# Two head pairs and a quarter of the frames in each step of an RWKV-7 recurrence, prepared further ahead

## The chip, the cores and the metric

The kernel runs on one core of one Trainium2 chip. The metric is device time in microseconds (us) for one execution, as a median over runs. Of the core's engines, TensorE (PE in the rows; PEld is its weight load) multiplies matrices into PSUM, VectorE (DVE) and ScalarE (ACT) work element by element and empty PSUM, GpSimd (POOL) helps with both kinds of elementwise work that touch no PSUM, and SyncE (SP) issues the DMAs, in the order in which they stand in the program.

## The reference

One residual block of a streaming encoder, on 1024 frames of 1024 channels, all in float32:

```python
h    = rmsnorm(x);  proj = h @ w_in                  # columns r | k | v | glu | gate logits
rkv  = rkv + (token_shift(rkv) - rkv) * mu_rkv
a    = rwkv7_mixer(h, r, k, v, ...)                  # 16 heads of 64, the recurrence below
c    = conformer_conv_mixer(glu)                     # GLU, causal depthwise conv of width 31, LayerNorm, silu
merged = gates[0] * (a @ w_rwkv_proj) + gates[1] * (c @ w_conv_proj)
x    = x + merged @ w_out
x    = x + square(relu(rmsnorm(x) @ w_ff1)) @ w_ff2
out  = rmsnorm(x)

def frame_step(S, r_t, w_t, k_t, v_t, kk_t, a_t):    # one head, S is 64 x 64
    sa = einsum('vk,k->v', S, -kk_t)
    S  = S * w_t + outer(sa, kk_t * a_t) + outer(v_t, k_t)
    return S, einsum('vk,k->v', S, r_t)
```

Decay `w_t`, rate `a_t` and the gate of the mixer come from small two-layer projections of h. Each head's output is normalised over its 64 channels, scaled, and given a bonus term of r, k and v.

## The kernel before

Activations lie channels by frames. A wide product is made of float32r products: both operands are split into a high and a low part, and each 128x128 block of weights (`whi`, `wlo`) is multiplied by 512 frames (`hhi`, `hlo`) three times. These are the "wide products" of the text: in the rows they write tile `g` and have form 128x512. Half a unit (four blocks, two segments of 512 frames) is 24 of them; a unit, 48, gives 128 columns of `w_in`.

The recurrence is computed in chunks of 64 frames. A head pair is 128 channels; two heads h lie on the partitions 0-63 and 64-127. There are 8 head pairs, and before the change a **step** i takes one head pair and half of the frames, that is 8 chunks, so there are 16 steps. For each step the following generators issue their work:

- `prep` makes decay products, the normalised key `kk` and the bonus `bn`. It reads k, r and v from SBUF, where `u_rkv` left them, and loads z and a (`z_d`, `al_d`) from DRAM. It contains two head sums (`headsum`, two 512-wide products each, tile `l`).
- `front` (twice per step, q = 0 and 1, four chunks each) transposes (`pt`) and makes for each head the products `pg` (4 calls of contraction 64, output 128x128). ScalarE and VectorE empty them into `lt`, `pl` and `mr`.
- `v_tm` transposes v (`pv`) into the tiles `sav` and `stv`.
- `invert` inverts the 64x64 triangular matrices of the step: 16x16 blocks by GpSimd, through DRAM (`scr_l`, `scr_x`, `scr_z`), and then TensorE (`pi`, `px`, `pz`, `pt2`, `pz2`).
- `chain` carries the state over the chunks, one after the other. Per chunk, for two heads: `ps1 = pl x stv` and the first half of the output `po = pr x stv`; VectorE copies ps1 to `rs`, and ScalarE makes `stw = stv * wc`; `ps2 = z x rs`, which VectorE copies into `sav`; `ps3 = bkt x sav`, from which VectorE makes the next state, `stv = ps3 * wc + stw`, and the second half of the output, `po += mr x sav`.
- `group_norm` normalises the output of the step (two head sums) and stores it (`a_d`).

The order of all engines in this stage is the order in which the program issues: a fixed dependency is added between an engine's consecutive instructions. The program goes through **ticks**. A step is NT = 24 ticks; `PLAN` says at which tick of which step a generator starts, each `yield` is one tick, and `chain` uses three ticks per chunk. After the generators of a tick, `large` issues wide products until the priced work of TensorE reaches TICK = 1800 (ns by a price list in the program) times the number of ticks, and `conv_ops` issues operations of the depthwise convolution on VectorE until its priced work has used a share DSHARE = 0.75 of the tick, at most two per tick. So the wide products (the columns r, k, v, glu and gates of `w_in`) fill the time in which the recurrence waits. Wide products not needed at a certain time (gates) go last; what is left of them is used after the recurrence. Before the loop of steps there are only four ticks for the second layer of the decay and rate projections (`second_layer`, tile `za`).

PSUM: three banks for the wide products, one for head sums, two (`mp`, tag "m") for all tiles of front, v_tm and invert, one for ps1 to ps3 and one for po.

## Time and profile before

| | |
|---|---|
| median of 3 runs | 2155.57 us (2146.05 to 2156.53) |
| profiled execution | 2136.36 us, its span 2134.6 us |
| TensorE busy in the span | 2030.9 us (95%) |
| VectorE, ScalarE, GpSimd busy | 1670.5 us (78%), 1086.4 us (51%), 667.5 us (31%) |
| stretch of the chain, from the end of step 0 to that of step 15 | 278 to 1124 us |

In the rows below, "idle before" is the time in which an engine had nothing running ahead of an instruction, and "<-" names what ended it. Matmuls are pipelined and their ends are modelled; the distance of two starts is the time that the first one takes, and a busy share says little. All instructions carry the line of one helper (L114), so groups are told apart by the tiles that they write and read. The span is the time from the first to the last instruction; 1.8 us lie around it.

### The profile page before, as it was taken

Reading aid. Unit: us, or ns where it says so; the run is one execution under the profiler, and the core shown is the slowest. Engines: PE = TensorE matmul, PEld = TensorE weight load, DVE = VectorE, ACT = ScalarE, POOL = GpSimd, SP = SyncE. Lnnn points to the kernel's source line nnn. Section 1 sums busy time; section 2 is a strip of 40 time slices with the busy share of each in tenths; the row PEclk is TensorE's granted clock in tenths of the full one; section 3 lists DMA queues with packets and bytes.
Section 4 is the critical chain, followed back from the end, with each engine's and each line's share of the span. In section 5 each row is a group of like instructions: output and inputs, shape, how many; then the busy total and the mean of one; then the engine's idle time right before and its main releaser. Section 6 shows DMA issues by size and latency. Waiting matters only on the chain.

```text
span 2134.6 us, 35368 instructions
## 1 busy us (share of the span) xinstructions
PE 2030.9 (95%) x12806; PEld 1538.7 (72%) x12806; DVE 1670.5 (78%) x2966; ACT 1086.4 (51%) x2046; POOL 667.5 (31%) x869
## 2 busy tenths in 40 slices
PE   6999999999999999999999999999999999999997
PEld 4767667677676666666667678777888887788886
DVE  8445989869868888888856697888676778999965
ACT  7564556555565565565433484557344445343423
POOL 4103433333332333433411222011122224455541
PEclk9999999999999999999999999999999999999999
DMA  5253222322222323222316336343544448454412
GB/s 183 76 190 79 55 60 68 85 70 80 76 74 65 90 64 83 74 84 74 91 58 217 133 134 203 133 142 134 174 143 153 153 162 265 144 165 144 124 45 79
DMA packets 235456, 246.91 MB, mean 116 GB/s; under 512 B 114833, under 2 KB 132753, under 8 KB 235281
## 3 DMA queue, kind: packets, MB, share of 16 engines
q1 hardware_dynamic: 235280, 244.65, 36.2%
q8 instruction: 101, 1.65, 0.3%
q14 instruction: 75, 0.61, 0.1%
HBM read 166.97 MB, written 77.61 MB: 115 GB/s over the span
## 4 chain that ended last, share of the span: by engine, by line
PE 65%; DVE 17%; issue 4%; DMA 4%; ACT 4%; POOL 3%; SPq 1%; POOLq 0%; DVEq 0%; ACTq 0%
PE g L114 37%; PE x L114 16%; DVE c L114 3%; PE pc L114 3%; PE pg L114 2%; DVE fa L114 2%; PE l L114 1%; PE pi L114 1%; PE po L114 1%; POOL xb L114 1%; POOL tmpb L114 1%; DMA xz<-scr_x 1%; PE pt L114 1%; DVE place L114 1%; ACT L114 1%
## 5 line engine op out<-in xcount | busy, mean ns | idle before, releaser
L114 POOL TENSOR_TENSOR wlo<-raw,whi 128x512 fp32r<-128x512 f32 x188 | 269.7, 1435 | 804.5 <-ACT whi L114 755.8
L114 PE MATMUL g<-hhi,whi 128*128 128x512 f32 x912 | 400.0, 439 | 0.0
L114 PE MATMUL g<-hhi,wlo 128*128 128x512 f32 x912 | 362.6, 398 | 2.1 <-POOL wlo L114 1.5
L114 PE MATMUL g<-hlo,whi 128*128 128x512 f32 x912 | 363.1, 398 | 0.0
L114 ACT ACTIVATE whi<-raw 128x512 fp32r<-128x512 f32 x328 | 205.0, 626 | 244.4 <-PE g L114 118.4
L114 PEld LDWEIGHTS g<-hhi,whi 128*128 128x128 f32 x912 | 172.6, 189 | 48.8 <-issue 1.9
L114 PE MATMUL g<-place,whi 128*128 128x512 f32 x640 | 202.4, 396 | 5.4 <-ACT place L114 3.7
L114 PEld LDWEIGHTS g<-hhi,wlo 128*128 128x128 f32 x912 | 173.3, 190 | 44.4 <-POOL wlo L114 2.4
L114 PE MATMUL x<-place,whi 128*128 128x512 f32 x624 | 195.9, 394 | 1.5 <-ACT place L114 0.9
L114 PEld LDWEIGHTS g<-hlo,whi 128*128 128x128 f32 x912 | 173.5, 190 | 27.3 <-issue 1.9
L114 PE MATMUL g<-a,whi 128*128 128x512 f32 x608 | 189.7, 393 | 2.7 <-ACT whi L114 1.4
L114 DVE TENSOR_TENSOR wlo<-raw,whi 128x512 fp32r<-128x512 f32 x140 | 100.7, 720 | 104.9 <-ACT whi L114 104.5
L114 PE MATMUL x<-a,whi 128*128 128x512 f32 x528 | 166.1, 396 | 10.7 <-DVE c L114 7.4
L114 PEld LDWEIGHTS g<-place,whi 128*128 128x128 f32 x640 | 120.4, 188 | 35.0 <-ACT place L114 4.1
L114 PEld LDWEIGHTS x<-place,whi 128*128 128x128 f32 x624 | 116.7, 188 | 30.1 <-ACT place L114 1.3
L114 PEld LDWEIGHTS g<-a,whi 128*128 128x128 f32 x608 | 113.6, 188 | 30.2 <-ACT whi L114 3.0
L114 ACT ACTIVATE stw<-stv,wc 64x64 f32<-64x64 f32 x240 | 82.5, 344 | 98.7 <-DVE stv L114 95.3
L114 POOL TENSOR_TENSOR tmpb<-lb,xb 64x15 f32<-64x15 f32 (+7 forms) x240 | 107.2, 447 | 80.4 <-DMA lb<-scr_l 64.2
L114 PE MATMUL g<-place,wlo 128*128 128x512 f32 x320 | 125.5, 392 | 0.6 <-DVE wlo L114 0.6
L114 PEld LDWEIGHTS x<-a,whi 128*128 128x128 f32 x528 | 99.0, 190 | 37.0 <-ACT whi L114 5.1
L114 PE MATMUL x<-place,wlo 128*128 128x512 f32 x312 | 122.0, 391 | 0.0
L114 PE MATMUL g<-a,wlo 128*128 128x512 f32 x304 | 119.0, 391 | 1.8 <-DVE wlo L114 1.0
(291 smaller groups left out, 4188.5 us busy)
## 6 DMA issues: line engine op xcount, KB each, us to landing
raw<-wf SPq DMA_DIRECT2D x128, 256.0 KB, 2.9
raw<-win SPq DMA_DIRECT2D x124, 256.0 KB, 3.0
f_d<-c SPq DMA_DIRECT2D x92, 256.0 KB, 2.3
fl<-f_d SPq DMA_DIRECT2D x76, 256.0 KB, 3.2
c<-f_d SPq DMA_DIRECT2D x30, 256.0 KB, 3.0
xt<-xT SPq DMA_DIRECT2D x16, 256.0 KB, 5.3
ga_d<-gt SPq DMA_DIRECT2D x16, 256.0 KB, 2.1
z_d<-za SPq DMA_DIRECT2D x16, 256.0 KB, 2.1
```

What stands on the lines that cost most here:

```text
L114: ins = f(*a, **k)
```

## The change

- A step takes **two head pairs and a quarter of the frames** (256 frames, 4 chunks of each pair). There are still 16 steps of 24 ticks, and the tiles of a step keep their size. `chain` now takes six ticks per chunk, and works on both pairs in each: every group of products has four calls in place of two, and the copies of VectorE take both pairs in one instruction (128x128 for `rs`, 64x2x64 for `sav` and `stv`). Operations with a scale per channel (in `prep` and `group_norm`) become two instructions of half the width.
- The state's decayed part is no longer made by ScalarE (`stw`). The state is added in PSUM by a product of the identity with `stv`, ahead of each product of ps3, and VectorE multiplies the sum by `wc`.
- k, r and v are stored to DRAM (`rkv_d`) by `u_rkv` and fetched by `prep`, as z and a are; `rp` has one buffer per name in place of three, and two for what `u_rkv` makes. The arrays in DRAM are laid out by two pairs, and a fetch or store has 128 x 2 runs of 256 frames.
- In `front` the products of the two heads alternate, and both tiles `pg` are made in one tick.
- `prep` starts at tick -6 of its place in place of 1, the other starts move too, and in `invert` there are nine ticks in place of two between the load of the inverted blocks and their first product, and four in place of two before GpSimd starts. Yields are added so that nearly all products of the generators fall in even ticks. Five buffers in place of four for `pr`, `bkt`, `pl`, `mr`.
- TICK is 1690 in place of 1800, the units of k, r and v are due at fixed ticks, and `conv_ops` issues up to three operations in even ticks and one in odd ones. Before the steps there is a loop that runs until v of pair 1 is made, with convolution operations in it; the first glu units stand ahead of it in the queue.

```diff
+QF = 256
 NSEG = 2
 NCH = 8
 CW = 31
-TICK = 1800.0
+TICK = 1690.0
 GAP = 1700.0
 DSHARE = 0.75
 NT = 24
-W_LB = 2
-W_XZ = 2
+W_LB = 4
 N_SUB = 2
...
                                              in1=sh[:, 0:SEG], op0=ALU.mult, op1=ALU.add)
                     if s == 0:
                         dve.tensor_copy(last, sh[:, SEG : SEG + 1])
-                    RKV[which, NSEG * p + s] = t
+                    sync.dma_start(rkv_d[which][p // 2][p % 2][:, s * SEG : (s + 1) * SEG], t)
+                    made.add((which, p, s))
...
+        def quarter(d, i):
+            return d[i // 4].rearrange("e p t -> p e t")[:, :, (i % 4) * QF : (i % 4 + 1) * QF]
+
+        def two(ap):
+            return ap.rearrange("p (e t) -> p e t", e=2)
...
+        def block(e, c):
+            return 4 * e + c
+
+        def fetched(which, i):
+
+            pp, u = divmod(i, 4)
+            need(which, 2 * pp, u // 2)
+            need(which, 2 * pp + 1, u // 2)
+            t = rp.tile([P, SEG], F32, tag=which, name=which)
+            sync.dma_start(two(t), quarter(rkv_d[which], i))
+            return t
...
             E = D[i] = {"q": [{}, {}]}
-            k = RKV["k", i]
+            k = fetched("k", i)
             sg, ta = t2k("sg"), t2k("ta")
-            sync.dma_start(sg, z_d[p][:, sl])
-            sync.dma_start(ta, al_d[p][:, sl])
+            sync.dma_start(two(sg), quarter(z_d, i))
+            sync.dma_start(two(ta), quarter(al_d, i))
+            yield
             sq = t2k("sq")
-            act.activation(sq, k, AF.Square, scale=v("kk", p))
+            for e, p in enumerate(P2):
+                act.activation(two(sq)[:, e], two(k)[:, e], AF.Square, scale=v("kk", p))
             yield
             hs = parts(sq)
             wt = sp.tile([P, NCH, 65], F32, tag="wt", name="wt")
...
+            r = fetched("r", i)
...
+            E["v"] = fetched("v", i)
...
         def front(i, q):
             E = D[i]
             bk, Q = E["bk"], E["q"][q]
+            blocks = [block(e, 2 * q + c) for e in range(2) for c in range(2)]
             if q == 1:
                 E["probe"](1)
-                done.add(("r", i))
             pt = mp.tile([P, 4, P], F32, tag="m", name="pt")
-            for j in range(4):
-                pe.transpose(pt[:, j, :], bk[:, 4 * q + j, :, :].rearrange("p a t -> p (a t)"), ident)
+            for j, b in enumerate(blocks):
+                pe.transpose(pt[:, j, :], bk[:, b, :, :].rearrange("p a t -> p (a t)"), ident)
             yield
             pr = Q["pr"]
...
                 E["lt"] = sp.tile([P, NCH, 64], F32, tag="lt", name="lt", bufs=2)
             lt = E["lt"]
             yield
-            mr = Q["mr"] = qp.tile([P, 2, 4, 64], F32, tag="mr", name="mr")
-            qs = slice(4 * q, 4 * q + 4)
+            yield
+            yield
...
-                for j in range(4):
-                    pe.matmul(pg[:, j, :], bk[rows, 4 * q + j, :, :].rearrange("p a t -> p (a t)"),
+
+            pgs = [mp.tile([P, 4, P], F32, tag="m", name="pg") for h in range(2)]
+            for j, b in enumerate(blocks):
+                for h, rows in enumerate((H0, H1)):
+                    pe.matmul(pgs[h][:, j, :], bk[rows, b, :, :].rearrange("p a t -> p (a t)"),
                               pr[rows, j, :, :].rearrange("p a t -> p (a t)"), start=True, stop=True)
-                yield
-                act.activation(lt[rows, qs, :], pg[H0, :, 0:64], AF.Copy)
+            yield
+            for h, rows in enumerate((H0, H1)):
+                pg = pgs[h]
+                act.activation(half(lt[rows], q), by_pair(pg[H0, :, 0:64]), AF.Copy)
                 dst = pl[H1, 0] if h == 0 else pl[H0, 1]
                 dve.tensor_tensor(out=dst, in0=pg[H1, :, 0:64], in1=mk(0, H1), op=ALU.mult)
                 dve.tensor_tensor(out=mr[:, h], in0=pg[:, :, 64:128], in1=mk(1, slice(0, 128)), op=ALU.mult)
@@ -860,9 +896,7 @@
             sync.dma_start(xb, eye16)
             for h in range(2):
                 sync.dma_start(mat(sl_, h), lt[64 * h : 64 * h + 64])
-            lm = sp.tile([P, NCH, 64], F32, tag="lm", name="lm")
...
-            for _ in range(W_XZ):
+            for _ in range(9):
                 yield
+            lm = sp.tile([P, NCH, 64], F32, tag="lm", name="lm")
+            dve.tensor_tensor(out=lm, in0=lt, in1=m16.unsqueeze(1).to_broadcast([P, NCH, 64]), op=ALU.mult)
+            yield
...
+                pc = chp.tile([P, 3, 2, 64], F32, tag="c", name="pc")
                 ps1, ps2, ps3 = pc[:, 0], pc[:, 1], pc[:, 2]
+                for e in pairs:
+                    for h in range(2):
+                        pe.matmul(ps1[hr[h], e], Q["pl"][:, h, 2 * e + cc, :], stv[:, h, 2 * e + cc, :],
+                                  start=True, stop=True)
+                rs = sp.tile([P, 2, 64], F32, tag="rsb", name="rsb", bufs=2)
+                dve.tensor_copy(rs, ps1)
+
+                for e in pairs:
+                    for h in range(2):
+                        pe.matmul(po[hr[h], block(e, c), :], stv[hr[h], h, 2 * e + cc, :],
+                                  Q["pr"][hr[h], 2 * e + cc, 1, :], start=(e == 0), stop=False,
+                                  skip_group_check=True)
+                yield
+                yield
+                for e in pairs:
+                    for h in range(2):
+                        pe.matmul(ps2[hr[h], e], z[hr[h], block(e, c), :], rs[hr[h], e], start=True, stop=True)
                 for h in range(2):
-                    pe.matmul(ps1[hr[h]], Q["pl"][:, h, j, :], Q["stv"][:, h, j, :], start=True, stop=True)
-                rs = sp.tile([P, 64], F32, tag="rsb", name="rsb", bufs=2)
-                dve.tensor_copy(rs, ps1)
-                for h in range(2):
-                    pe.matmul(po[hr[h], c, :], Q["stv"][hr[h], h, j, :], Q["pr"][hr[h], j, 1, :],
-                              start=True, stop=False)
-                last = s == NSEG - 1 and c == NCH - 1
-                if not last:
-                    stw = sp.tile([P, 64], F32, tag="stw", name="stw", bufs=2)
-                    for h in range(2):
-                        act.activation(stw[hr[h]], Q["stv"][hr[h], h, j, :], AF.Copy,
-                                       scale=wc[hr[h], c, 0:1])
+                    dve.tensor_copy(sav[0:64, cc:4:2, 64 * h : 64 * h + 64], ps2[hr[h]])
                 yield
-                for h in range(2):
-                    pe.matmul(ps2[hr[h]], z[hr[h], c, :], rs[hr[h]], start=True, stop=True)
-                dve.tensor_copy(Q["sav"][0:64, j, 0:64], ps2[0:64])
-                dve.tensor_copy(Q["sav"][0:64, j, 64:128], ps2[64:128])
                 yield
-                if not last:
-                    for h in range(2):
-                        pe.matmul(ps3[hr[h]], Q["bkt"][:, j, 64 * h : 64 * h + 64],
-                                  Q["sav"][:, j, 64 * h : 64 * h + 64], start=True, stop=True)
-                    if c < NCH - 1:
-                        nq, nj = divmod(c + 1, 4)
+                if not (u == 3 and c == 3):
+                    for e in pairs:
+                        for h in range(2):
+                            pe.matmul(ps3[hr[h], e], ident[:, 64 * h : 64 * h + 64], stv[:, h, 2 * e + cc, :],
+                                      start=True, stop=False)
+                            pe.matmul(ps3[hr[h], e], Q["bkt"][:, 2 * e + cc, 64 * h : 64 * h + 64],
+                                      sav[:, 2 * e + cc, 64 * h : 64 * h + 64], start=False, stop=True)
+                    if c < 3:
+                        nq, nc_ = divmod(c + 1, 2)
                         nstv = E["q"][nq]["stv"]
                     else:
-                        nj, nstv = 0, D[i + 1]["q"][0]["stv"]
+                        nc_, nstv = 0, D[i + 1]["q"][0]["stv"]
                     for h in range(2):
-                        dve.scalar_tensor_tensor(out=nstv[hr[h], h, nj, :], in0=ps3[hr[h]],
-                                                 scalar=wc[hr[h], c, 0:1], in1=stw[hr[h]],
-                                                 op0=ALU.mult, op1=ALU.add)
-                for h in range(2):
-                    pe.matmul(po[hr[h], c, :], Q["sav"][:, j, 64 * h : 64 * h + 64], Q["mr"][:, h, j, :],
-                              start=False, stop=True)
-                if c == NCH - 1:
+                        dve.tensor_tensor(out=nstv[hr[h], h, nc_:4:2, :], in0=ps3[hr[h]],
+                                          in1=wc[hr[h], c:8:4, :].to_broadcast([64, 2, 64]), op=ALU.mult)
+                for e in pairs:
+                    for h in range(2):
+                        pe.matmul(po[hr[h], block(e, c), :], sav[:, 2 * e + cc, 64 * h : 64 * h + 64],
+                                  Q["mr"][:, h, 2 * e + cc, :], start=False, stop=True, skip_group_check=True)
+                if c == 3:
...
+        queue.append((passed(), [u_rkv(0, "k"), u_rkv(1, "k"), decay_and_a] + glu_units(0) +
+                      [u_rkv(e, x) for x in "rv" for e in range(2)] + [gate_lora]))
+        tick = [0]
+        for pp in range(1, NK // 2):
+            for j, (x, e) in enumerate((x, e) for x in "krv" for e in range(2)):
+                due = NT * (4 * pp - 4) + 15 * j
+                queue.append((lambda due=due: tick[0] >= due, [u_rkv(2 * pp + e, x)]))
...
-        PLAN = [(1, 2, prep), (24, 0, group_norm), (15, 2, front0), (24, 2, front1), (35, 2, v_tm), (29, 2, invert)]
+        PLAN = [(-6, 2, prep), (24, 0, group_norm), (10, 2, front0), (12, 2, front1), (28, 2, v_tm), (18, 2, invert)]
...
-        for _ in range(4):
-            next(za)
+        while ("v", 1, 1) not in made:
+            next(za, None)
             large(pe.work + TICK)
+            conv_ops(2, dve.work + TICK * DSHARE)
         pe0 = pe.work
-        for i in range(-2, NI + 1):
-            if i == -2:
-                live = [(len(PLAN), za)]
+        live = [(len(PLAN), za)]
+        for i in range(-3, NI + 1):
...
-                conv_ops(2 if i < NI - 2 else 3, d0 + TICK * (DSHARE if i < NI - 2 else 1.0) - behind)
+                share = DSHARE if i < NI - 2 else 1.0
+                conv_ops(3 - 2 * (t % 2), d0 + TICK * (share + (-0.35 if t % 2 else 0.35)) - behind)
```

## Rows read from the trace of the kernel before

**Rows 1.** The page: busy time of each engine, granted clock, chain of work by engine

```profile
PE 2030.9 (95%) x12806; PEld 1538.7 (72%) x12806; DVE 1670.5 (78%) x2966; ACT 1086.4 (51%) x2046; POOL 667.5 (31%) x869
...
PEclk9999999999999999999999999999999999999999
...
PE 65%; DVE 17%; issue 4%; DMA 4%; ACT 4%; POOL 3%; SPq 1%; POOLq 0%; DVEq 0%; ACTq 0%
```

**Rows 2.** Windows: stretch, length, busy us of PE, PEld, DVE, ACT, POOL, clock, DMA

```profile
100.00:278.00 178.00, 165.81 (x1106) 123.75 (x1106) 109.63 (x218) 92.95 (x177) 44.35 (x83) 0.98 0.34 106
278.00:1124.00 846.00, 815.89 (x7214) 579.96 (x7209) 697.25 (x1480) 466.27 (x988) 292.19 (x543) 0.99 0.27 74
```

**Rows 3.** Timeline of TensorE at 357 us: start, us, engine, operation, tiles

```profile
357.25 0.40 PE L114 MATMUL g<-hlo,whi 128*128 128x512 f32 x1
357.49 0.40 PE L114 MATMUL g<-hhi,wlo 128*128 128x512 f32 x1
357.82 0.33 PE L114 MATMUL pc<-rsb,z 64*64 64x64 f32 x4
358.08 0.50 PE L114 MATMUL g<-hhi,whi 128*128 128x512 f32 x1
```

**Rows 4.** Timeline of TensorE at 464 us

```profile
463.87 0.34 PE L114 MATMUL pc<-stv,pl 128*64 128x64 f32 x4
464.14 0.33 PE L114 MATMUL po<-pr,stv 64*64 64x64 f32 x4
464.40 0.49 PE L114 MATMUL g<-hhi,whi 128*128 128x512 f32 x1
464.73 0.39 PE L114 MATMUL g<-hlo,whi 128*128 128x512 f32 x1
```

**Rows 5.** Timeline of TensorE at 523 us

```profile
523.36 0.39 PE L114 MATMUL g<-hhi,wlo 128*128 128x512 f32 x1
523.68 0.34 PE L114 MATMUL pc<-sav,bkt 128*64 128x64 f32 x4
523.84 0.29 PE L114 MATMUL po<-mr,sav 128*64 128x64 f32 x4
524.06 0.50 PE L114 MATMUL g<-hhi,whi 128*128 128x512 f32 x1
```

**Rows 6.** Timeline of TensorE at 601 us, two ticks without a wide product between

```profile
600.87 1.16 PE L114 MATMUL pg<-pr,bk 64*128 64x128 f32 x8
601.95 0.34 PE L114 MATMUL pc<-stv,pl 128*64 128x64 f32 x4
```

**Rows 7.** Timeline of TensorE at 887 us

```profile
887.18 1.10 PE L114 MATMUL pi<-xz,lm 64*64 64x64 f32 x32
888.21 0.50 PE L114 MATMUL g<-hhi,whi 128*128 128x512 f32 x1
```

**Rows 8.** Groups of TensorE by form, 278 to 1124 us: busy, mean ns, idle before

```profile
L114 PE MATMUL pc<-stv,pl 128*64 128x64 f32 x480 | 40.4, 245 | 13.6 <-DVE stv L114 13.3
...
L114 PE MATMUL pi<-xz,lm 64*64 64x64 f32 x896 | 34.5, 223 | 6.1 <-DMA xz<-scr_x 4.7 <-DVE mr L114 0.6 <-issue 0.6
```

**Rows 9.** Groups of VectorE by form, 278 to 1124 us

```profile
L114 DVE SCALAR_TENSOR_TENSOR fa<-u,cws,fa 128x512 f32<-128x512 f32 x107 | 87.3, 816 | 1.9
...
L114 DVE SCALAR_TENSOR_TENSOR stv<-pc,wc,stw 64x64 f32<-64x64 f32 x226 | 63.9, 283 | 46.2 <-PE pc L114 40.8
L114 DVE COPY sav<-pc 64x64 f32<-64x64 f32 x240 | 52.4, 218 | 22.1 <-PE pc L114 19.6
...
L114 DVE TENSOR_TENSOR pl<-pg,cst 64x256 f32<-64x256 f32 x54 | 23.1, 427 | 6.8 <-ACT lt L114 5.5
```

**Rows 10.** DMA issues: tiles, count, size, median us from issue to landing

```profile
sg<-z_d SPq DMA_DIRECT2D x16, 256.0 KB, 4.7
```

**Rows 11.** Timeline of SyncE's queue at 602 us

```profile
601.96 0.57 SPq L114 DMA_DIRECT2D a_d<-o  x1
```

**Rows 12.** Windows of tile gt alone (gate units): busy us of VectorE, ScalarE

```profile
1100.00:1210.00 110.00, 0.00 (x0) 9.60 (x14) 0.98 0.50 170
```

More of the change, by code (lines that the diff above doesn't have):

```diff
@@ L752, in prep @@
             rkk = t2k("rkk")
-            dve.scalar_tensor_tensor(out=rkk, in0=r, scalar=v("rk", p), in1=k2, op0=ALU.mult, op1=ALU.mult)
+            for e, p in enumerate(P2):
+                dve.scalar_tensor_tensor(out=two(rkk)[:, e], in0=two(r)[:, e], scalar=v("rk", p),
+                                         in1=two(k2)[:, e], op0=ALU.mult, op1=ALU.mult)
             yield
@@ L782, in v_tm @@
                 pe.transpose(pv[:, w, :], vv[:, w * P : (w + 1) * P], ident)
-            done.add(("v", i))
             yield
@@ L1008, in group_norm @@
             yield
+            yield
             ps = headsum(*hs)
@@ L1023, in group_norm @@
             yield
-            dve.scalar_tensor_tensor(out=o, in0=o, scalar=v("lxg", p), in1=bn, op0=ALU.mult, op1=ALU.add)
+            for e in range(2):
+                dve.scalar_tensor_tensor(out=two(o)[:, e], in0=two(o)[:, e], scalar=v("lxg", 2 * (i // 4) + e),
+                                         in1=two(bn)[:, e], op0=ALU.mult, op1=ALU.add)
             yield
-            sync.dma_start(a_d[p][:, sl], o)
+            for e in range(2):
+                sync.dma_start(a_d[2 * (i // 4) + e][:, (i % 4) * QF : (i % 4 + 1) * QF], two(o)[:, e])
         convs = []
@@ L1093, in conv, with need @@
             done.add(("c_d", p))
-        queue.append((passed(), [u_rkv(0, "k"), decay_and_a, u_rkv(0, "r"), u_rkv(0, "v"), gate_lora]))
-        for p in range(NK):
-            if p:
-                i = NSEG * p + NSEG - 1 - 3
-                queue += [(passed((n, i)), [u_rkv(p, n)]) for n in "krv"]
-        queue += [(lambda p=p: p == 0 or ("conv", p - 1) in done, glu_units(p)) for p in range(NK)]
+        queue.append((passed(), [u_rkv(0, "k"), u_rkv(1, "k"), decay_and_a] + glu_units(0) +
[5 more added lines that the diff above has]
+                queue.append((lambda due=due: tick[0] >= due, [u_rkv(2 * pp + e, x)]))
+        queue += [(lambda p=p: ("conv", p - 1) in done, glu_units(p)) for p in range(1, NK)]
         queue += [(passed(), [gate_unit(n, (1,) if n < EARLY else (0, 1))]) for n in range(2 * NK)]
         advance(8)
-        def need(which, i):
-            while (which, i) not in RKV:
+        def need(which, p, s):
+            while (which, p, s) not in made:
                 next(G)
```

102 lines of the change are left out of this document (51 added, 51 removed).

## The prediction

> **What bounds the kernel now.** I read the page first. TensorE is busy for 95% of the span, its granted clock is at the upper level (2.4 GHz) in all 40 slices as rounded, and the chain that ended last lies for 65% on TensorE [rows 1]. So a microsecond is won where TensorE is spared it, and another engine counts only where TensorE waits for it. Then the windows: the change touches the stretch of the chain, 278 to 1124 us, and what lies just ahead of it. In that stretch TensorE is busy for 816 of 846 us and VectorE for 697, or 82% [rows 2]: VectorE is next in line. The chain's 15 steps in it take 56.4 us each, 2.35 us per tick, though a tick is priced at 1.8.
>
> Where the difference goes is seen only in the timeline of TensorE, from start to start. A wide product takes 0.24 us when another follows (357.25 to 357.49). The one ahead of ps2 takes 0.33 (to 357.82): 0.10 more to change over. The two calls of ps2 take 0.26 until the next wide product (358.08) [rows 3]. In the product of 16 calls (32 instructions) a call costs 0.064 (1.03 us in all), and some 0.058 once 0.10 are taken off for the way out [rows 7]. So of those 0.26 us, 0.12 are calls and 0.14 the way back. The first wide product after a visit then takes 0.33 in place of 0.23 (464.40 to 464.73) [rows 4]. A **visit** to the small products thus costs 0.10 + 0.14 + 0.10 = 0.34 us beside the calls themselves. A change of form inside a visit costs too: from ps1 to po 0.27 us for two calls, 0.15 too much [rows 4]; from ps3 to po 0.16, nearly nothing [rows 5].
>
> **The change, part by part.** *Visits.* Before, the chain has products in all 24 ticks of a step. The two ticks of a `front` run together without a wide product between them [rows 6], which leaves 22 visits. After, it has products in the 12 even ticks, and by counting the yields the head sums, `pt`, `pg`, `pv`, `pi` and `pz` all fall in even ticks; only `px` and `pt2` are in odd ones. That makes 14 visits: 8 fewer x 0.34 x 16 steps = **-44 us**. There are also four po groups in place of eight: 4 x 0.15 x 16 = **-9 us**. The calls of chain, head sums and inverse are the same in number.
>
> *The identity product.* 240 more calls (16 steps x 4 chunks x 2 pairs x 2 heads, less the last chunks). The cheap end is 0.058 us each, 14 us [rows 7]. The dear end: calls of one head follow each other now, state and identity, and if they don't overlap with the other head's, both cost as `pg` does per column, where one head works alone: 1.08 us for 8 instructions of 128 columns [rows 6], or 0.135 for a call of 64; 240 x 0.135 + 240 x (0.135 - 0.058) = 51 us. The nearest row is ps3 itself, 0.16 us for two calls [rows 5], so I take 0.08 each: **+20 us**. The Trainium skill, "TensorE: Matmul & The Clock Gate", section "Part 3: Packing small matmuls — row/col tiling", speaks against this edit: a weight load overlaps a running matmul only if it is for other rows of the array, and identity and state products take all 128 rows. By it the dear end would hold; ps3 takes all rows too, and at 0.16 us for two calls it doesn't yet show it.
>
> *`pg`.* 64 groups (16 steps, two fronts, two heads) of 1.08 us [rows 6]. Before, the four calls of a head follow each other on the same 64 rows; after, the heads alternate, on different rows and into different PSUM tiles. No row shows this form overlapped; the chain's and the inverse's pairs, which differ in columns as well, show it (a call at 0.058, against 0.135 above) [rows 6, 7]. Some 0.2 us of a group are way in and out, 0.88 can halve: 64 x 0.44 = 28 us. The bounds are 0 and, with the group's fixed part saved too, -35. I take **-28**, since both known pairs overlap. The Trainium skill, "TensorEngine Tiling (Array Packing)", section "Restrictions and Gotchas", says that parts of the array that differ in rows must write different PSUM banks; the change has a bank for each head, so by that rule too they may run together.
>
> *Waits of TensorE.* ps1 waits 13.6 us for the state, mostly for VectorE, and `pi` 6.1 for the inverse's load [rows 8]. After, there are two ticks from one group of the chain to the next, and nine from the load to `pi`: **-15 us** (0 to -20).
>
> *VectorE.* In place of ten instructions for two chunks (two rs, four sav, four stv) it has five, of double width. From sav at 0.218 us and stv at 0.283 [rows 9], 64 columns more should add some 0.07 (an estimate from these: 512 columns take 0.816), so five of 0.29 to 0.35 take 1.6 us where ten took 2.4: 64 x 0.8 = 51 us less work, and ScalarE is spared stw, all beside TensorE's work. But a tick becomes shorter, and the work now comes in heaps. By the starts in `PLAN`, `front` 0 has `pg` in tick 14 and `front` 1 in tick 16. Both need both banks of `mp`, so TensorE in tick 16 waits until VectorE has emptied the first two, issued in tick 15. Ahead of these four operations of 0.43 stand, from tick 14, two sav copies (0.6), one of `group_norm` (0.8) and two of the convolution (0.8 each) [rows 9]: 4.7 us after ps2. TensorE needs some 1.0 us for the first `pg`, 1.6 for seven wide products and 1.0 for ps3 and po, 3.7 in all, and waits 1.0. `pi` in tick 18 needs a bank emptied in tick 17, behind three convolution operations, and by the same count waits 1 to 1.6. Before, consecutive users of a bank were likewise a tick apart, but ticks were 2.35 us long and no tick had three. Bounds 0 (convolution done, which frees a third of the steps) and 3.5 us x 16 = 56; I take 1.25 a step, **+20 us**.
>
> *Fetches.* k is fetched one tick before ScalarE squares it. The fetch of z, of the same size, takes 4.7 us from issue to landing [rows 10], a tick will be about 2. ScalarE stands for 2.7 us with all that is queued behind it: the high parts of weights, and copies out of PSUM. The weights' half unit in use covers 24 x 0.23 = 5.5 us [rows 3], so little reaches TensorE: **+6 us**, from 0 to 16 x 2.8 = 45. r and v have three ticks and more. The stores of r, k and v and the shorter runs load the DMA engines, which are at a share of 0.27 in this stretch [rows 2]: nothing.
>
> *Pace.* TICK 1690 and the dearer price of the state product leave about 20 fewer wide products to a step. They aren't gone: some six units move ahead of the steps. TensorE's sum doesn't change by it, as long as wide products remain: 14 of 26 gate segments come after 1100 us [rows 12], 14 x 24 x 0.23 = 77 us of cover. If that cover were gone, `large` would find nothing, and each missing tick would cost up to 1.7 us. The convolution begins ahead of the steps, where VectorE is busy for 110 of 178 us [rows 2].
>
> The sum: -44 - 9 + 20 - 28 - 15 + 20 + 6 = **-50 us**. The profiled execution took 2136.4 us, its span 2134.6, so it would take 2086. The median of the runs is 19 us above it (2155.6); the same 50 us off that median give **2106 us**.
>
> **The rivals.**
> 1. *Everything falls well.* No wait for VectorE or for k, the identity at its cheap end, `pg` halved in full: -44 - 9 + 14 - 35 - 20 = -94, **2062 us**. For it: VectorE idles now mostly for TensorE's sake [rows 9], and the last third of the steps has no convolution.
> 2. *The identity is dear* (the rule above): 31 more, **2137 us**.
> 3. *VectorE becomes the bound*, by the two banks of `mp`: 3.5 us in each of 19 steps, 66 in place of 20, **2152 us**. For it: 82% busy, in ticks to be made shorter by a sixth; against it: 51 us less work.
> 4. *The change doesn't do what it says*: alternating heads don't overlap and the identity is dear: -50 + 28 + 31 = +9, **2165 us**.
> 5. *Slower: SyncE's queue.* It issues in order, one DMA in 0.57 us [rows 11], and a step has 7 more (three fetches, three stores, one more of `a_d`), each behind waits for its data; the weights of the wide products are loaded by the same queue, two half units ahead, 11 us. Once a store that waits holds the queue for longer than these 11 us, TensorE stands. If each new issue then costs its time, 16 x 7 x 0.6 = 67 us: +17, **2173 us**. Against it: the loads ahead cover today's waits.
>
> **How the numbers follow.** The forecast has a chance of 0.46 (its own range 2080 to 2130); rival 1 0.17, rival 2 0.08, rival 3 0.12, rival 4 0.07, rival 5 0.10. Half a per cent is 10.8 us, about what a measurement of this kernel can tell from no change: faster is below 2144.8, slower above 2166.4. Forecast and rivals 1 and 2 are faster (0.71), with 0.04 of rival 3: 0.75. Same: the rest of rival 3 and most of rival 4, 0.14. Slower: 0.11. The range leaves out rival 5, rival 4 and the lower edge of rival 1: 2055 to 2156.
>
> **What would show it.** In the trace after: a step of some 48 us in the stretch of the chain; one visit in two ticks; `pg` of 16 instructions in 1.1 to 1.3 us (right) or 2.0 (wrong); ps3 with the identity at 0.6 to 0.7 us for eight calls (right) or 1.1 (dear); idle time of `pg` and `pi` put down to VectorE near 20 us, 60 if rival 3 holds; weights waited for by TensorE, if rival 5 does. What would make it wrong most easily is the price of VectorE's heaps, which no row of before shows.

## The result, and the profile after

The changed kernel takes 2122.39 us (median of 4 runs, 2120.38 to 2125.8), the kernel before 2155.07 beside it (2146.05 to 2156.53): a ratio of 0.9874, 95% interval 0.985 to 0.9898. 32.7 us were gained where 50 were forecast; the time lies inside the range. The profiled execution's span went from 2134.6 to 2119.4 us only, by 15: the execution profiled before lies 19 us below its median, the one after 1 us. So sums by spans, below, make every gain over the kernel before some 10 to 18 us smaller than the ratios do.

The page of the kernel after, busy time and granted clock, as in [rows 1]:

```profile
PE 1974.4 (93%) x13286; PEld 1543.2 (73%) x13286; DVE 1613.0 (76%) x2702; ACT 1043.2 (49%) x1864; POOL 648.2 (31%) x861
...
PEclk9999998999999999999999999999999999999999
...
PE 44%; DVE 11%; ACT 3%; issue 3%; DMA 2%; POOL 1%; POOLq 0%; DVEq 0%; ACTq 0%; SPq 0%
```

TensorE has 57 us less to do and VectorE 58. But the share of TensorE fell, so it waits more, and the clock row has an 8 for the first time. The shares of the last chain can't be set beside those of before: they add up to 64% here and to 98% there, since the chain after is followed back only to 730 us. Of what was followed, TensorE still has two thirds in both. Now the windows of the kernel after, in the form of [rows 2]: ahead of the chain's first step, its 15 steps to the end of the last, and what follows.

```profile
0.00:360.00 360.00, 323.31 (x1809) 250.21 (x1809) 237.65 (x425) 171.84 (x303) 87.28 (x124) 0.96 0.40 127
360.00:1117.00 757.00, 692.52 (x7332) 526.58 (x7326) 584.42 (x1142) 405.74 (x779) 258.14 (x524) 0.95 0.36 100
1117.00:2119.00 1002.00, 958.59 (x4158) 766.37 (x4157) 790.94 (x1136) 465.61 (x783) 302.73 (x214) 0.99 0.46 150
```

In the stretch of the chain a step takes 50.5 us in place of 56.4 (48 were forecast). Most of this is no gain: 1584 wide products lie in the stretch in place of 1880, some 20 fewer to a step as forecast, and at 0.23 us these make 68 of the 88 us by which it is shorter; they now stand ahead of it. One of their three groups by form, of the kernel before and after, in these stretches:

```profile
L114 PE MATMUL g<-hhi,whi 128*128 128x512 f32 x627 | 279.3, 446 | 0.0
L114 PE MATMUL g<-hhi,whi 128*128 128x512 f32 x528 | 230.6, 437 | 1.4 <-ACT whi L114 1.4
```

The granted clock of the stretch is 0.95 where it was 0.99, and TensorE is idle for 64.5 us, 8.5% of it, where it was 30. Who is waited for, from TensorE's groups by form in the same stretch, as in [rows 8]:

```profile
L114 PE MATMUL pi<-xz,lm 64*64 64x64 f32 x896 | 39.1, 250 | 26.7 <-issue 26.7
...
L114 PE MATMUL pg<-pr,bk 64*128 64x128 f32 x416 | 34.6, 289 | 12.4 <-DVE mr L114 12.4
...
L114 PE MATMUL l<-hsh,bonr 128*128 128x512 f32 x56 | 27.9, 497 | 10.6 <-ACT gsq L114 7.4 <-DVE sq L114 3.1
L114 PE MATMUL pc<-stv,pl 128*64 128x64 f32 x480 | 27.6, 237 | 0.7 <-DVE stv L114 0.5
...
L114 PE MATMUL px<-lm,xz 32*32 32x32 f32 x448 | 12.6, 218 | 7.6 <-ACT lm L114 7.6
```

The wait of ps1 for the state is gone, 0.7 us where it was 13.6. In its place stand `pi`, `pg`, `l` and `px`, 57 us in all. "Issue" behind `pi` names no releaser; the timeline of one step shows what stands there. TensorE from 899.93 on, and VectorE beside it (start, us, engine, operation, tiles, idle time before):

```profile
899.93 0.45 PE L114 MATMUL po<-mr,sav 128*64 128x64 f32 x8
901.59 0.46 PE L114 MATMUL pg<-pr,bk 64*128 64x128 f32 x2 [1.22 <-DVE mr L114]
902.49 1.13 PE L114 MATMUL pg<-pr,bk 64*128 64x128 f32 x14 [0.44 <-DVE mr L114]
...
904.83 0.45 PE L114 MATMUL po<-pr,stv 64*64 64x64 f32 x8
907.36 1.37 PE L114 MATMUL pi<-xz,lm 64*64 64x64 f32 x32 [2.08 <-issue]
909.42 1.06 PE L114 MATMUL px<-lm,xz 32*32 32x32 f32 x32 [0.69 <-ACT lm L114]
910.41 0.80 PE L114 MATMUL g<-hhi,whi 128*128 128x512 f32 x1
911.01 0.63 PE L114 MATMUL g<-hlo,whi 128*128 128x512 f32 x1
911.43 0.63 PE L114 MATMUL g<-hhi,wlo 128*128 128x512 f32 x1
```

```profile
899.14 0.74 DVE L114 SCALAR_TENSOR_TENSOR fa<-u,cw,fa 128x512 f32<-128x512 f32 x1
899.80 0.74 DVE L114 SCALAR_TENSOR_TENSOR fb<-u,cw,fb 128x512 f32<-128x512 f32 x1
900.58 0.43 DVE L114 TENSOR_TENSOR pl<-pg,cst 64x256 f32<-64x256 f32 x1
901.02 0.42 DVE L114 TENSOR_TENSOR mr<-pg,cst 128x256 f32<-128x256 f32 x1
...
901.92 0.42 DVE L114 TENSOR_TENSOR mr<-pg,cst 128x256 f32<-128x256 f32 x1
...
906.24 0.42 DVE L114 TENSOR_TENSOR mr<-pg,cst 128x256 f32<-128x256 f32 x1
906.58 0.68 DVE L114 TENSOR_TENSOR lm<-lt,cst 128x512 f32<-128x512 f32 x1
907.18 0.28 DVE L114 COPY rsb<-pc 128x128 f32<-128x128 f32 x1
```

The second front's `pg` starts when VectorE has emptied the first bank (901.02 to 901.44, 901.59), and again after the second: it stands behind two operations of the convolution. `pi` starts at 907.36, right behind `lm` (to 907.26), which stands behind the four operations that empty `pg`'s banks, and these again behind two of the convolution. Then the windows of the same place:

```profile
897.00:908.00 11.00, 7.26 (x103) 5.62 (x102) 10.78 (x24) 2.14 (x5) 0.00 (x0) 1.00 0.50 150
908.00:915.00 7.00, 6.31 (x88) 5.03 (x85) 2.32 (x6) 3.11 (x6) 1.10 (x1) 0.51 0.46 124
```

In the 11 us of the waits VectorE is busy for 10.78 and TensorE for 7.26, at a granted clock of 1.00. Just behind them the clock is 0.51, the lower level (1.2 GHz), for 7 us: a wide product starts 0.42 us after the one before it (911.01 to 911.43) in place of 0.23. In the stretch of the chain the records show 13 such pieces of 3.4 to 10.2 us, 75 us together (the expectations below put it at 89), where the kernel before has two (10 us). By 0.42 and 0.23 us, about half of such time is lost: some 32 us of the 65 that were added.

### The profile page after: what moved, and what is told of

The parts are those of the page before. It is cut to its first block, busy times and chain, and to the rows that moved or that the text cites. A ratio compares the mean times of both kernels' runs of the same rounds, so it can differ in the third digit from the quotient of the medians.

```text
span 2119.4 us, 36050 instructions
## 1 busy us (share of the span) xinstructions
PE 1974.4 (93%) x13286; PEld 1543.2 (73%) x13286; DVE 1613.0 (76%) x2702; ACT 1043.2 (49%) x1864; POOL 648.2 (31%) x861
## 4 chain that ended last, share of the span: by engine, by line
PE 44%; DVE 11%; ACT 3%; issue 3%; DMA 2%; POOL 1%; POOLq 0%; DVEq 0%; ACTq 0%; SPq 0%
PE g L114 24%; PE x L114 16%; DVE c L114 3%; DVE fa L114 2%; PE pc L114 1%; DVE place L114 1%; PE pi L114 1%; ACT L114 1%; PE l L114 1%; DVE wlo L114 1%; DVE a L114 1%; DMA y<-a_d 1%; DMA ga<-ga_d 0%; PE po L114 0%; PE pg L114 0%
## 5 line engine op out<-in xcount | busy, mean ns | idle before, releaser
L114 PE MATMUL g<-hhi,whi 128*128 128x512 f32 x912 | 387.8, 425 | 1.9 <-ACT whi L114 1.9
L114 PE MATMUL g<-hhi,wlo 128*128 128x512 f32 x912 | 368.3, 404 | 5.3 <-POOL wlo L114 4.2
L114 PE MATMUL g<-hlo,whi 128*128 128x512 f32 x912 | 368.0, 404 | 0.0
L114 DVE TENSOR_TENSOR c<-c,g 128x512 f32<-128x512 f32 (+1 forms) x131 | 84.8, 651 | 39.7 <-PE g L114 39.5
L114 POOL TENSOR_TENSOR tmpb<-lb,xb 64x15 f32<-64x15 f32 (+7 forms) x240 | 99.5, 415 | 42.3 <-DMA lb<-scr_l 27.1
```

The costliest lines, as they stand in the source:

```text
L114: ins = f(*a, **k)
```

## The experiments

The theories, drawn from these rows. **A:** VectorE's heap in ticks 14 to 17 makes `pg` and `pi` wait, and the waits, in a row of small products, bring the lower clock; both go when VectorE's order in these ticks changes, though its work stays. **B:** the denser row of small products alone lowers the clock. **C:** `pi` waits for the inverse's DMAs. And the prediction's **rival 3:** VectorE as a whole is the bound.

All kernels in one table. Ratio is to the kernel before, run beside each (95% interval; its median was 2145 to 2147 us beside all but the second row). Waits: TensorE's idle time before its products; lower: time with a granted clock at the lower level; both of the whole profiled execution, in us, followed by the part that lies in the 15 steps of the chain. Step: mean of these.

| kernel | ratio | span | step | waits | lower |
|---|---|---|---|---|---|
| before | 1 | 2134.6 | 56.4 | 95, 30 | 51, 10 |
| after | 0.9874 (0.985 to 0.9898) | 2119.4 | 50.5 | 136, 65 | 128, 75 |
| e1_lm_early | 0.9721 (0.969 to 0.9752) | 2084.2 | 48.5 | 122, 50 | 79, 38 |
| e2_conv_moved | 0.9725 (0.9682 to 0.9768) | 2086.7 | 48.4 | 118, 47 | 92, 41 |
| e3_both | 0.9591 (0.9565 to 0.9618) | 2055.3 | 46.5 | 103, 36 | 55, 3 |
| e4_heads_apart | 0.9891 (0.9862 to 0.992) | 2118.7 | 50.5 | 122, 53 | 132, 79 |
| e5_po_apart | 0.9652 (0.963 to 0.9674) | 2067.0 | 47.3 | 92, 20 | 36, 3 |
| e6_stw_back | 0.973 (0.9701 to 0.9758) | 2082.1 | 49.0 | 133, 52 | 92, 24 |
| e7_tick_1800 | 0.9656 (0.9633 to 0.9679) | 2067.3 | 49.1 | 117, 34 | 72, 7 |
| e8_l_px | 0.9781 (0.9749 to 0.9814) | 2098.4 | 49.4 | 125, 53 | 78, 41 |
| e9_tick_1600 | 0.9666 (0.9644 to 0.9688) | 2075.2 | 45.1 | 115, 42 | 72, 27 |
| e10_pg_apart_e3 | 0.9624 (0.96 to 0.9647) | 2063.3 | 47.0 | 98, 29 | 51, 10 |
| e11_l_alone | 0.9677 (0.9645 to 0.9709) | 2075.8 | 47.9 | 121, 49 | 51, 14 |

**e1_lm_early.** The copy `lm` six ticks earlier, where VectorE has no heap:

```
-            for _ in range(9):
+            for _ in range(3):
                 yield
             lm = sp.tile([P, NCH, 64], F32, tag="lm", name="lm")
             dve.tensor_tensor(out=lm, in0=lt, ...)
-            yield
+            for _ in range(7):
+                yield
```

> The changed kernel, with the masked copy lm of the inverse issued in tick 11 of the step in place of tick 17, where it stands behind the four operations that empty the second front. Theory A (TensorE waits at pi for VectorE, for lm itself, and the clock falls to its lower level after such waits): the waits of pi fall from 26.7 us in the stretch of the chain to about 8 (the PSUM bank that pi needs is still emptied late), the time at the lower clock from 89 us to 50 to 70, and the median from 2122 to 2090 to 2105 us. Theory B (the clock falls because of the small products of ticks 14 to 19 themselves, whatever they wait for): the waits fall likewise, the lower clock stays at 80 to 90 us, median 2104 to 2108. Theory C (pi waits for the DMA of the inverse): the waits stay above 20 us and the median at 2120 to 2125.

The median fell to 2087.51 us. `pi` waits 8.6 us in place of 26.7, `pg` 15.0 in place of 12.4; the lower clock halves to 38 us. C asked for waits above 20 us, so it falls. The lower clock and the median fell further than A said.

**e2_conv_moved.** No operation of the convolution in ticks 14 and 16; the other ticks take them:

```
+                share = min(1.0, share + 0.15)
-                conv_ops(3 - 2 * (t % 2), d0 + TICK * ...
+                conv_ops(0 if t in (14, 16) else 3 - 2 * (t % 2), d0 + TICK * ...
```

> The changed kernel without convolution operations in ticks 14 and 16 of each step; the others get a share of 0.90 in place of 0.75, so that the convolution ends at about the same time. Theory A: the waits of pg fall from 12.4 to under 4 us and those of pi from 26.7 to under 12, the lower clock from 89 to 30 to 60 us, the median to 2065 to 2095 us. Theory B: the same waits, the lower clock still 75 us or more, median 2095 to 2105. If VectorE's whole load is the bound and not its heaps (rival 3 of the prediction), the waits only move to other ticks and the median stays within 2112 to 2130.

2087.3 us. Here `pg` waits 3.5 us as A said, but `pi` 19.2 where under 12 were expected: `lm` still stands where it stood, which alone, in e1_lm_early, took 18 us off `pi`.

**e3_both.** Both edits.

> Both edits: lm in tick 11 and no convolution operations in ticks 14 and 16. Theory A: waits of pg and pi together under 8 us (39 before), lower clock under 40 us, median 2055 to 2085 us. Theory B: waits as small, lower clock 70 us or more, median 2085 to 2100. VectorE's whole load as the bound: above 2105.

2058.51 us (2057.21 to 2062.94), 4.1% under the kernel before and the best of all. The windows of its chain stretch, and the groups of TensorE in it:

```profile
353.00:1051.00 698.00, 661.84 (x7361) 504.33 (x7358) 571.60 (x1122) 407.35 (x780) 272.57 (x520) 1.00 0.38 108
```

```profile
L114 PE MATMUL pg<-pr,bk 64*128 64x128 f32 x416 | 33.8, 286 | 6.1 <-DVE mr L114 5.2 <-DVE sh L114 0.9
...
L114 PE MATMUL pi<-xz,lm 64*64 64x64 f32 x896 | 31.0, 219 | 2.8 <-ACT lt L114 1.9 <-issue 0.8
L114 PE MATMUL l<-hsh,bonr 128*128 128x512 f32 x56 | 28.1, 502 | 13.9 <-DVE sq L114 7.1 <-ACT gsq L114 6.8
```

The waits of `pg` and `pi` are 8.9 us together, just above the 8 of A. The clock of the stretch is 1.00, with VectorE's work nearly that of the kernel after (571.6 and 584.4 us) in a stretch that is 59 us shorter: its load is 82% now, and rival 3 falls. The same small products stand in 12.8 visits to a step as in the kernel after, so B falls too. A holds: between the two kernels 64 us of span; 33 of them are waits (136 to 103) and 36 are half of 73 us at the lower clock (128 to 55). The sum, 69, is 5 too much. By the ratios the two kernels differ by 61 us.

**e4_heads_apart.** From the kernel after, the heads of `pg` one after the other again:

```
-            for j, b in enumerate(blocks):
-                for h, rows in enumerate((H0, H1)):
+            for h, rows in enumerate((H0, H1)):
+                for j, b in enumerate(blocks):
                     pe.matmul(pgs[h][:, j, :], ...
```

> The changed kernel, with the products pg of the two heads one head after the other again, four calls each, all else as changed. If alternating heads overlap (the term of 28 us in the sum): 16 instructions of pg take about 2.0 us in place of 1.13, and the median rises by 20 to 30 us from 2122, unless the wait for VectorE at the next front shrinks by as much, since VectorE gets 0.9 us more per front; then by 5 to 15 us. If they don't overlap: no change, 2118 to 2126.

No change, 2123.53 us, as for heads that don't overlap. The timeline of TensorE shows that they do, though the 16 instructions take 1.64 us where 2.0 were expected; the kernel after first, then this one (the product behind `pg` starts 1.09 and 1.64 us after it):

```profile
438.73 1.16 PE L114 MATMUL pg<-pr,bk 64*128 64x128 f32 x16
439.82 0.49 PE L114 MATMUL g<-hhi,whi 128*128 128x512 f32 x1
```

```profile
438.09 1.71 PE L114 MATMUL pg<-pr,bk 64*128 64x128 f32 x16
439.73 0.50 PE L114 MATMUL g<-hhi,whi 128*128 128x512 f32 x1
```

32 x 0.55 = 17.6 us more of products, and 14 us less of waits (136 to 122): a longer `pg` fills most of the time in which TensorE would wait for VectorE.

**e10_pg_apart_e3.** The same edit on e3_both, where little waits.

> From e3_both, the two heads of pg one after the other again, as in e4_heads_apart, where the 0.55 us more for 16 instructions were taken out of waits that TensorE had anyway. Here the waits of pg and pi are 9 us in place of 39. Theory (the alternation is worth 32 x 0.55 us where nothing else waits): +12 to +18 us, ratio 0.964 to 0.968. Rival (it is absorbed here too): within 4 us.

+0.3%, or 7 us: between the two, and the intervals of the two kernels overlap. The span grew by 8, the waits fell by 6 and the lower clock by 4; so by this sum the alternation is worth 8 + 6 + 2 = 16 us, near the 17.6 of the timeline, and even here a third of it is taken out of waits.

**e5_po_apart.** From e3_both, the products of `po` in the odd ticks:

```
                 dve.tensor_copy(rs, ps1)
+                yield
                 for e in pairs:
                     for h in range(2):
                         pe.matmul(po[hr[h], block(e, c), :], ...
                 yield
-                yield
...
                         dve.tensor_tensor(out=nstv[hr[h], h, nc_:4:2, :], ...
+                yield
                 for e in pairs:
                     for h in range(2):
                         pe.matmul(po[hr[h], block(e, c), :], ...
...
                 yield
-                yield
```

> From e3_both. The calls of po, on which no later step of the chain waits, move to the odd tick behind ps1 and behind ps3: same calls, same chain, but up to 8 more visits in each of 16 steps (128), and the change of form from ps1 to po (0.15 us, 64 times) goes. Theory (a visit costs 0.34 us beside its calls, the first term of the prediction): 128 x 0.34 - 10 = +34 us against e3_both, ratio to before about 0.975, and some 20 visits to a step in the trace. Rival (visits cost little, and the gain of the change came from the waits for the state that went with the wider tick): under +12 us, ratio below 0.965.

+0.6%, 13 us by the ratios and 12 of span: a miss, with the rival's 12 much nearer than the theory's 34. Two things lie behind it. There are 17.3 visits to a step, 72 more in all and not 128, since some odd ticks get no wide product between. And the waits fell by 11 us and the lower clock by 19, so the visits cost 12 + 11 + 9 = 32 us net, 0.45 each; with the 10 us expected for the change of form, which is gone everywhere in the stretch, it is 42, or 0.58. Such sums leave 5 to 10 us unplaced in other runs here, so the price of a visit is shown as 0.34 or more, and not better. Lone visits show the term that was read: eight instructions alone take 0.38 us from start to start here.

```profile
602.25 0.40 PE L114 MATMUL g<-hhi,wlo 128*128 128x512 f32 x1
602.58 0.45 PE L114 MATMUL po<-pr,stv 64*64 64x64 f32 x8
602.96 0.49 PE L114 MATMUL g<-hhi,whi 128*128 128x512 f32 x1
603.29 0.39 PE L114 MATMUL g<-hlo,whi 128*128 128x512 f32 x1
```

The way in costs 0.10 us (602.25 to 602.58 in place of 0.23), the calls and the way back 0.38, the first wide product 0.10 more: with four calls at 0.058 that is 0.10 + 0.15 + 0.10, as in [rows 3].

**e6_stw_back.** From e3_both, the state scaled by ScalarE as before, no identity product (and one buffer for `rs` in place of two):

```
+                            act.activation(stw[hr[h], e], stv[hr[h], h, 2 * e + cc, :], AF.Copy,
+                                           scale=wc[hr[h], block(e, c), 0:1])
...
-                            pe.matmul(ps3[hr[h], e], ident[:, 64 * h : 64 * h + 64], ...
...
-                        dve.tensor_tensor(out=nstv[hr[h], h, nc_:4:2, :], in0=ps3[hr[h]], ...
+                            dve.scalar_tensor_tensor(out=nstv[hr[h], h, 2 * e + nc_, :], in0=ps3[hr[h], e],
+                                                     scalar=wc[hr[h], block(e, c), 0:1], in1=stw[hr[h], e], ...
```

> From e3_both. The state is scaled by ScalarE again (four copies of 64x64 a chunk) and the identity calls of TensorE go; VectorE makes the new state in four instructions of 64x64 in place of two of 64x128. TensorE loses 240 calls at 0.065 us, 16 us, if the identity is priced as its trace says; VectorE gets some 120 us... of instructions in 16 steps that now take 0.28 each in place of 0.29 (two more a chunk, 64 x 2 x 0.28 = 36 us), which TensorE sees only where it waits for VectorE. Theory (identity cheap, VectorE's heaps decide): between -16 us and +10 us against e3_both, waits of TensorE in the stretch above 36 us. Rival (identity dear, as the prediction's upper bound had it): -30 us or more.

+30 us by the ratios: outside what either theory said. Its head sum among TensorE's groups by form in the stretch of the chain, and the windows of that stretch:

```profile
L114 PE MATMUL l<-hsh,bonr 128*128 128x512 f32 x56 | 28.0, 500 | 35.0 <-ACT gsq L114 28.7 <-DVE sq L114 6.0
```

```profile
357.00:1092.00 735.00, 682.83 (x7027) 514.88 (x7026) 611.23 (x1254) 486.06 (x1014) 265.24 (x524) 0.98 0.37 106
```

ScalarE has 79 us more to do in the stretch, VectorE 40, and the head sum `l` waits 28.7 us for ScalarE in place of 6.8. Span +27, of it waits +30 and half of the lower clock +18: TensorE itself is spared 21 us, near the forecast's 20 for the identity. So the edit that was costed at +20 is a gain of about 27 on e3_both. But not all of it is what the edit takes off ScalarE and VectorE. Without the identity's price, `large` puts 114 more wide products into the stretch and leaves 120 fewer behind it, and 18 of the 48 us of waits and lower clock lie there (12 + 6), as when the pace is 1800 (next). In the stretch it is 16 + 10 = 26 us against the 21 that TensorE is spared. With the cover held, which was not tried, the gain may be as small as 5 to 9 us.

**e7_tick_1800, e9_tick_1600.** From e3_both, the pace alone: `TICK` 1800 and 1600 in place of 1690.

> From e3_both, the pace set back from 1690 to 1800. Theory (the pace moves wide products between places and TensorE's sum stays): within 6 us of e3_both, ratio 0.956 to 0.962; steps longer by some 1.5 to 2.5 us in the stretch of the chain, and as much less behind it; waits for VectorE fall a little, by up to 8 us, since ticks are longer. Rival (the shorter tick is itself part of the gain): slower by 10 us or more.

> From e3_both, the pace shortened from 1690 to 1600. In e7_tick_1800, 167 wide products more lay in the stretch of the chain and 206 fewer behind it, where TensorE then waited 54 us in place of 35. Theory (what the pace is worth is the cover behind the chain, which is enough at 1690): within 6 us of e3_both, ratio 0.956 to 0.962, some 130 wide products fewer in the stretch, waits behind it 30 to 35 us, waits in it up by up to 10 us. Rival (a shorter tick keeps paying as from 1800 to 1690): -8 us or more.

Both are slower, by 0.7 and 0.8%, some 14 and 16 us. For 1800 the rival held (10 us or more), for 1600 neither: 1690 is better than both. At 1800 the wide products behind the chain are 206 fewer, and TensorE waits there for 54 us in place of 35, with 52 us at the lower clock in place of 28. At 1600 waits rise both in the chain (42 in place of 36) and behind it (41), and the lower clock by 17 us in all; half of that and the waits' 11.5 are the 20 us of span exactly. For 1800 the same sum gives 22 where 12 were measured; the other 10 I can't place.

**e8_l_px, e11_l_alone.** From e3_both, two waits more taken away, then the first alone:

```
             parts_lo(*hs)
             yield
-            yield
-            yield
             ps = headsum(*hs)
...
-            for _ in range(3):
+            for _ in range(5):
                 yield
```

```
             act.activation(t1, ps, AF.Copy)
             yield
+            yield
             px = ...
```

> From e3_both, two waits more taken away: the second head sum of the group norm two ticks earlier, so that ScalarE has read its bank before the next head sum wants it (l waits 14.1 us in e3_both, 6.8 of it for ScalarE), and px one tick later, so that ScalarE has copied lm by then (7.6 us). Theory (what is left of the waits is lost time): waits of TensorE in the stretch near 22 us in place of 36, -8 to -14 us, ratio near 0.954. Rival (another wait takes their place, or the moved products make visits of their own): within 4 us of e3_both.

> From e3_both, of the two edits of e8_l_px only the head sum two ticks earlier. In e8_l_px the wait moved from px to pz (17.6 us, for ScalarE, behind a row of small products), and the lower clock came back right behind it (41 us in 11 pieces, against 3.4 in one). Theory (px alone did it; l only changes the engine it waits for): within 5 us of e3_both, at most 2 pieces at the lower clock in the stretch. Rival (the head sum did it): +20 us or more, and 5 pieces or more.

Both misses. The earlier head sum costs 18 us by itself: it no longer waits for ScalarE, but for VectorE's low part of its input, 12.2 us, and `l` waits 19.4 us in all in place of 14.1. The chain's products wait 5 us more for VectorE too; the rest of the 18 is not placed. And `px` a tick later (some 22 us more) waits no more, but pushes the rest of the inverse by a tick, where `pz` stands right behind `pt2` and ScalarE's copy of it. TensorE's timeline of e8_l_px, and `pz` among its groups by form:

```profile
845.42 0.69 PE L114 MATMUL pt<-xz,lt 32*32 32x32 f32 x32
847.10 0.24 PE L114 MATMUL pz<-z,lm 32*32 32x32 f32 x2 [0.98 <-ACT lm L114]
...
848.11 0.50 PE L114 MATMUL g<-hhi,whi 128*128 128x512 f32 x1
```

```profile
L114 PE MATMUL pz<-z,lm 32*32 32x32 f32 x480 | 14.3, 197 | 17.6 <-ACT lm L114 15.0 <-DVE stv L114 2.4
```

With a wait of 1.0 us or more in most steps at this place, 41 us of the lower clock come back, in 11 pieces, eight of which begin at it or up to 1.8 us behind it. In the stretch e8_l_px is 43 us longer than e3_both: 17 are waits, 19 half of the lower clock, 7 not placed. In e11_l_alone three pieces (14 us) were there where at most two were expected.

## Why the prediction was right, and where it was not

The sum came out 16 us from the median, but it was split the wrong way, and that the time lies so near is in part luck: two errors of opposite sign stand in it. TensorE's own saving was larger than forecast, and most of it went into two things, one under-sized, one not in the sum. Against e3_both the kernel before is 79 us longer in span, though its waits are 8 us and half of its lower clock 2 us less; so the edits to TensorE's work are worth about 90 us, where the forecast's terms without waits gave 61. From the kernel before to the one after, waits grew by 41 us and half of the lower clock by 39, where the forecast had +11 for all waits and nothing for the clock.

- **Visits, -44.** Right in kind, low in size. 12.8 in a step of the stretch in place of 21.9, nine fewer where eight were counted; at the 0.34 us read these are 49 us, at the 0.45 to 0.58 of e5_po_apart 65 to 84. "One visit in two ticks" held. The changes from ps1 to po, -9, halved as said: 60 in the stretch in place of 120.
- **Identity, +20.** Right: 16 to 21 us. Four pairs of calls of ps3 take 0.52 us in the kernel after, 0.065 a call (timeline of TensorE, with two of its weight loads):

```profile
899.41 0.34 PE L114 MATMUL pc<-stv,cst 128*64 128x64 f32 x4
899.52 0.21 PEld L114 LDWEIGHTS pc<-sav,bkt 128*64 128x64 f32 x4
899.58 0.29 PE L114 MATMUL pc<-sav,bkt 128*64 128x64 f32 x4
899.64 0.25 PEld L114 LDWEIGHTS pc<-stv,cst 128*64 128x64 f32 x4
899.69 0.34 PE L114 MATMUL pc<-stv,cst 128*64 128x64 f32 x4
899.81 0.34 PE L114 MATMUL pc<-sav,bkt 128*64 128x64 f32 x4
```

  (899.41 to 899.93, below the 0.6 to 0.7 forecast.) Rival 2 falls. The rule of the Trainium skill, "TensorE: Matmul & The Clock Gate", section "Part 3: Packing small matmuls — row/col tiling", that a weight load overlaps a running matmul only for other rows, does not agree with these rows: all calls take all 128 rows and differ in columns only, and the loads start (899.52, 899.64) while the products before them run. What failed here is the sentence that ScalarE is spared "beside TensorE's work": on e3_both the relief is worth at least what the calls cost (e6_stw_back).
- **`pg`, -28.** Right in mechanism: 1.09 us for 16 instructions, where two groups took 1.08 each [rows 6]. By these rows that is 32 x (2.16 - 1.09) = 34 us, the upper bound. The alternation by itself is 16 to 18 of it (e4_heads_apart, e10_pg_apart_e3); the other half comes from the two groups standing together (2.16 to 1.64 in e4_heads_apart), and some of that is counted among the visits. The Trainium skill, "TensorEngine Tiling (Array Packing)", section "Restrictions and Gotchas", has different row tiles write to different PSUM banks; the two heads do, and overlap (1.09 against 1.64 us). In the kernel after, nothing of the alternation reaches the end, since waits take it.
- **Waits for the state and for the inverse's load, -15.** Right: 13.6 to 0.7 us, and no wait for a DMA is left at `pi`.
- **VectorE's heaps, +20.** The step that failed, and the one that the prediction called its weakest. The place and the cause were named rightly (`pg` in tick 16, `pi` in tick 18, the four operations of the banks behind the convolution), but `pi`'s count had left out `lm`, which the change moves to tick 17, behind those four, and on which `pi` waits directly. `pg` and `pi` wait 39 us, `l` and `px`, never counted, 18. The test "20, or 60 if rival 3 holds" could not tell the two apart: 39 lies midway, and 57 with `l` and `px`, but VectorE's load was not the bound; its order was (e3_both, with the same work).
- **The clock.** Not in the sum at all, some 32 us in the stretch and 39 in the whole. It was the largest omission. No row of before priced it, but two pieces at the lower level stood there too, beside waits of `pi`.
- **Fetches, +6.** Nothing of it is seen at TensorE: ScalarE waited three times for k, 10.9 us in all, once in the stretch (3.3 us). Its fetch takes 3.8 us from issue to landing (DMA issues of the kernel after: count, KB each, median us):

```profile
k<-k_d SPq DMA_DIRECT2D x16, 256.0 KB, 3.8
```

- **Pace, 0.** Wrong in size: on e3_both, 1690 in place of 1800 is worth about 14 us. The cover behind the chain was the right question, but it was answered for the case that it is gone, and not for the waits that it hides while it shrinks.
- **Rivals 4 and 5** fall: the alternation and the identity work, and TensorE's waits for weights in the stretch rose only from 2 to 6 us. **Rival 1** (2062 us) is what e3_both shows, 2058.5, though by another sum: its TensorE terms were too small and its waits not gone.

## What to carry to other kernels

When a change packs more of one engine's products into fewer and shorter ticks, write out the other engine's queue for the two or three ticks where banks change hands, with every operation that the change moves there, and move what is not urgent before pricing the rest. Here two moves of VectorE's work, none of it less, were worth about twice the change itself. And price a wait on TensorE in a row of small products at more than its length: look for the granted clock right behind it.

## What the runs showed of the hardware

- Beside waits of 1 to 3.4 us between small products the granted clock fell to its lower level for 3.4 to 10.2 us at a time, nearly once in each step (13 pieces in 15 steps after, 12 of them at waits of `pg` or `pi`; eight at `pz` in e8_l_px). Waits of like size before `l`, a product of 512 columns, mostly did not bring it: of 12 waits of 1.6 to 3.4 us in e6_stw_back, four stand beside such a piece. What it is in the place that decides was not tried alone.
- Two products on different halves of the rows, alternating, take 1.09 us where one after the other they take 1.64: a gain of a third, not of half.
- A `visit` costs the same by the timeline, some 0.35 us beside its calls, whether four or eight instructions stand in it ([rows 3], e5_po_apart); by the sum of e5_po_apart it is dearer, and why stays open.
- Weight loads for products that take all 128 rows start while products on the same rows run (899.52 us): eight such calls of 64 columns take 0.52 us.
